# Sample queries: high and low parts side by side in the weight columns, one score pass instead of two

## The chip, the cores and the metric

One core of one Trainium2 chip runs one inference step of a hybrid encoder layer. The metric is the device time of one execution in microseconds (us). Everything is 32-bit; products that need full precision are made of high and low parts in a reduced format (the names ending in hi and lo, or the two halves of a tile called hl).

## The reference, cut to what matters

Two groups of rows go through one layer: 1024 prompt rows and 64 sample rows. The sample rows attend to a cache of 512 past rows and to themselves (8 "fox" heads with a forget bias), and to 256 memory rows (4 memory heads). Only this part is touched by the change:

```
def fox_attend(q, k, v, Fq, Fk, qpos, kpos):
    s = einsum('bqhd,bkhd->bhqk', q, k) * SCALE
    bias = Fq[..., :, None] - Fk[..., None, :]
    s = where(kpos[None, :] <= qpos[:, None], s + bias, NEG)
    p = softmax(s, axis=-1)
    return einsum('bhqk,bkhd->bqhd', p, v)

def mem_attend(qm, mk, mv):
    s = einsum('bqhd,bkhd->bhqk', qm, mk) * SCALE
    p = softmax(s, axis=-1)
    return einsum('bhqk,bkhd->bqhd', p, mv)

# sample rows: fox_attend(q, [ck, k], [cv, v], ...) with 512 + 64 keys, 64 queries
#              mem_attend(qm, cmk, cmv) with 256 keys, 64 queries
```

Around it lie a root-mean-square norm, one input projection, a pooling mixer, SiLU gates, an output projection with residual, and a final norm, for both groups.

## The kernel before, in words

A planner (class Planner, lines 43 to 253) collects all instructions of the kernel in program order, each with a modelled duration, and `flush` puts them into an order: at each step it takes the engine and the instruction that can start first; at equal times TensorE writes into the banks `ps`, `pt` and `po` go ahead of projections. Five engine queues then run in exactly that order. The planner also links the users of a buffer with the users of the next tile that takes the same buffer, and buffers of one tag are handed out in program order. There are two flushes: norms, values, memory keys and the first projections, then all the rest.

Data: `proj` (line 603) makes one 128-column tile of the input projection in three chunks of rows (256, 512 and 320, the last with the 64 sample rows); each chunk is 24 matmuls into a bank of the ring `pp` and an evacuation through a tile of the ring `row`, which has five buffers for the whole kernel (line 292). `q_tile` splits a query tile into high and low halves in a tile `hl` of two halves of 1152 columns, copies the 64 sample columns a second time beside themselves so that they fill 128 weight columns, and stores all four groups of 64 rows to DRAM (`qd`). `load_q` fetches a head's queries into two tiles, `qa` (prompt rows 0 to 511 and the doubled sample rows) and `qb`.

Attention: a head's keys (`ks`, or `km` for a memory head) lie as high part over low part on the 128 partitions, and the queries twice, so one matmul gives a product with both parts of the keys. `score` (line 834) runs two such passes into one bank, with the high and with the low half of the queries as weights. The scores go through the ring `s`, two banks, handed out in program order. `fox_sample` makes scores in two pieces of 288 keys, adds the bias and takes a running minimum on VectorE, takes the exponential on ScalarE, and `sample_pv` transposes 128 rows and multiplies with the values. Rows 64 to 127 repeat rows 0 to 63. `mem_sample` does the same with one piece of 256 keys and no bias. `fox_unit` and `mem_unit` treat four blocks of 256 prompt rows.

Order in the program: for each head of the list "f0:u0 qm0|f1:qm1|f2:q2 k2|f3:u1|m0:q3|m1:|m2:k3|m3:|f4:gf0 gf1|f5:gf2|f6:gf3 gp0|f7:gp1 gmx0" first the head (its loads, its sample part, its four blocks) and then the projections behind the colon (gates are `gate_tile`, with two `row` tiles per chunk; queries and keys take one). Behind the sample part of f7 and behind each of its blocks, `store_rinv` (line 857) transposes the softmax sums through a bank of the ring `pt` and takes one `row` tile. Then come the output projection's weights (`load_wout`) and nine output tiles (`out_tile`), the sample tile first.

Of the kernel before, what the change touches and what calls it, by code (L numbers as in the profile page):

```python
# [7 lines left out]
F32 = mybir.dt.float32  # L8
F32R = mybir.dt.float32r
BF16 = mybir.dt.bfloat16  # L10
AF = mybir.ActivationFunctionType
ALU = mybir.AluOpType
AX = mybir.AxisListType
# [16 lines left out]
CH = [(0, 256), (256, 512), (768, 320)]  # L30
LAST = (2, 1, 0)
NQ = NT + NSA
TQ, TK, TGF, TU, TGP, TQM, TGM = 0, 4, 8, 12, 14, 16, 18


# [237 lines left out]
def tile_hymba_step(  # L273
# [23 lines left out]
    def nm(s):  # L297
        uid[0] += 1
        return f"{s}_{uid[0]}"
# [10 lines left out]
    def row(name):  # L310
        return rp.tile([P, 512], F32, tag="row", name=nm(name))
# [4 lines left out]
    def mm(out, lhsT, rhs, start, stop):  # L316
        nc.tensor.matmul(out, lhsT=lhsT, rhs=rhs, start=start, stop=stop)
# [1 line left out]
    def half(par):  # L319
        return slice(64 * par, 64 * par + 64), slice(64 - 64 * par, 128 - 64 * par)  # L320

    qd = [dram.tile([4 * HD, 2, NQ], F32, name=f"qd{j}") for j in range(6)]
    kd = [dram.tile([4 * HD, NT + PAST], F32, name=f"kd{j}") for j in range(4)]
    md = [dram.tile([4 * HD, 2 * MEM], F32, name=f"md{j}") for j in range(2)]
    gated = [dram.tile([768, n], F32, name=f"gated_{t0}") for t0, n in CH]
# [291 lines left out]
    def halves():  # L617
        return rp.tile([P, 2, NQ], F32R, tag="hl", name=nm("hl"), bufs=HB)

    def split(hl, src, c0, n):  # L620
        hi, lo = hl[:, 0, c0 : c0 + n], hl[:, 1, c0 : c0 + n]
        nc.scalar.copy(hi, src)
        nc.gpsimd.tensor_tensor(lo, src, hi, op=ALU.subtract)

    def q_tile(j):
        hl = halves()

        def f(acc, ci, t0, n):
            t = row("qr")
            nc.vector.scalar_tensor_tensor(  # L630
                t[:, :n], acc[:, :n], SCALE, rb[:, t0 : t0 + n], op0=ALU.mult, op1=ALU.mult
            )
            if ci == 2:
                nc.vector.tensor_copy(t[:, n : n + NSA], t[:, n - NSA : n])
            for a, b, c in ((0, 512, 0), (512, NPR, P), (NPR, NQ, -512)):
                a, b = max(a, t0), min(b, t0 + n + (NSA if ci == 2 else 0))
                if a < b:
                    split(hl, t[:, a - t0 : b - t0], a + c, b - a)
            if ci == 2:
                for r in range(4):  # L640
                    nc.sync.dma_start(qd[j][r * HD : r * HD + HD], hl[r // 2 :: 2].bitcast(F32))

        return f

# [168 lines left out]
    def small(shape, tag):  # L813
        return ap_.tile(shape, F32, tag=tag, name=nm(tag), bufs=6)
# [5 lines left out]

    def load_q(j, par):
        out = []
        for tag, c0, n in (("qa", 0, 512 + P), ("qb", 512 + P, 512)):
            q = ap_.tile([P, 2, n], F32R, tag=tag, name=nm(tag), bufs=1)
            nc.sync.dma_start(q.bitcast(F32), qd[j][par * P : par * P + P, :, c0 : c0 + n])
            out.append(q)
        return out

    def q_part(q, c):
        t = q[c in (2, 3)]  # L830
        c0, n = ((0, 256), (256, 256), (0, 256), (256, 256), (512, P))[c]
        return t[:, 0, c0 : c0 + n], t[:, 1, c0 : c0 + n]

    def score(out, q, qs, kst, ks0, n):
        mm(out, q[0][:, qs], kst[:, ks0 : ks0 + n], True, False)
        mm(out, q[1][:, qs], kst[:, ks0 : ks0 + n], False, True)
# [9 lines left out]
    def softmax_tail(Pt, m, rows, n, rs, src=None):  # L846
        nc.scalar.activation(
            Pt[:rows, :n], Pt[:rows, :n] if src is None else src, AF.Exp, bias=m,
            scale=-1.0 if src is None else 1.0, accum_out=rs[:rows],
        )  # L850
# [3 lines left out]
    def rs_col(c, head, i=0):  # L854
        return rsum[:, c, 12 * i + head : 12 * i + head + 1]
# [104 lines left out]
    def fox_sample(h, ks, raw, q):  # L960
        par = h % 2
        j = h // 2
        n = PAST + NSA
        nb = nbt(5 * P)
        nc.sync.dma_start(
            nb[:, : 5 * P],
            gsd[5 * h : 5 * h + 5, :].rearrange("t p -> (t p)").unsqueeze(0).to_broadcast([P, 5 * P]),
        )
        nc.gpsimd.tensor_tensor(nb[:, PAST:n], nb[:, PAST:n], mask[:, :NSA], op=ALU.add)
        q = q_part(q, 4)  # L970
        Pt = ptile()
        nc.gpsimd.memset(Pt[:, n : n + NSA], 0.0)
        prev = BIG
        for a in (0, 288):
            s = pst()
            score(s[:, :288], q, slice(0, P), ks, NPR + a, 288)
            m = small([P, 1], "m")
            nc.vector.tensor_tensor_reduce(
                out=Pt[:, a : a + 288], in0=s[:, :288], in1=nb[:, a : a + 288],
                scale=-1.0, scalar=prev, op0=ALU.add, op1=ALU.min, accum_out=m,  # L980
            )
            prev = m
        softmax_tail(Pt, prev, P, n, rs_col(4, h))
        sample_pv(Pt, 5, raw, 7, par, j * P)

    def sample_pv(Pt, nt, raw, v0, par, row0):
# [68 lines left out]
    def mem_sample(h, km, raw, q):  # L1055
        par = h % 2
        j = h // 2
        q = q_part(q, 4)
        s = pst()
        score(s[:, :256], q, slice(0, P), km, MEM, 256)  # L1060
        m = small([P, 2], "m2")
        nc.vector.tensor_reduce(
            out=m[:, 0:1], in_=s[:, :256], axis=AX.X, op=ALU.max, negate=True
        )
        Pt = ptile(256)
        softmax_tail(Pt, m[:, 0:1], P, 256, rs_col(4, 8 + h), src=s[:, :256])
        sample_pv(Pt, 2, raw, 1, par, 768 + j * P)

    UW = 15 + NPR + 15 + NSA
# [81 lines left out]
    def out_prep(t):  # L1151
        m = P if t < 8 else NSA
        ci = 0 if t < 2 else 1 if t < 6 else 2
        o, oc = t * P - CH[ci][0], t % 2 * P
        kv = lambda x: x[:, :D].rearrange("p (k t) -> p k t", k=KT)
        hk = lambda x, w: x[:, : w * m].rearrange("p (k t) -> p k t", k=w)
        spare = order.index(t) % 3 == 2
        if spare:
            ch = ap_.tile([P, KT, P], F32R, tag="vs", name=nm("chi"))
        else:  # L1160
            ch = kv(wp.tile([P, WC], F32R, tag="whi", name=nm("chi")))
        if t < 8:
            if spare:
                cl = ap_.tile([P, KT, P], F32R, tag="vs", name=nm("clo"))
            else:
                cl = kv(wp.tile([P, WC], F32R, tag="wlo", name=nm("clo")))
        else:
            cl = ch[:, :, m:]
        w = 512 // m
        if order.index(t) % 2:  # L1170
            rt = ap_.tile([P, 2, 512 + P], F32, tag="qa", name=nm("rt"), bufs=1)
            rt = rt.rearrange("p a b -> p (a b)")
        else:
            rt = ap_.tile([P, 13, HD], F32, tag="vraw", name=nm("rt"), bufs=1)
            rt = rt.rearrange("p a b -> p (a b)")
        rt = rt[:, : 6 * m].rearrange("p (k t) -> p k t", k=6)
        for par in (0, 1):
            nc.sync.dma_start(
                rt[64 * par : 64 * par + 64],
                rsd[min(t // 2, 4)].rearrange("(i k a) t -> i a k t", i=2, a=2)[  # L1180
                    t % 2, par, :, :m
                ].unsqueeze(0).to_broadcast([64, 6, m]),
            )
        for a in range(0, KT, w):
            ct, gt = hk(ptile(512), w), hk(ptile(512), w)
            nc.sync.dma_start(
                ct, catd[t // 2][a * P : (a + w) * P, oc : oc + m].rearrange("(k p) t -> p k t", p=P)
            )
            e1 = min(a + w, 6)
            nc.sync.dma_start(  # L1190
                gt[:, : e1 - a, :],
                gated[ci][a * P : e1 * P, o : o + m].rearrange("(k p) t -> p k t", p=P),
            )
            ks = slice(a, a + w)
            for b0, b1, o0 in ((0, 4, 0), (6, 8, 2)):
                b0, b1 = max(a, b0), min(a + w, b1)
                if b0 < b1:
                    c_ = ct[:, b0 - a : b1 - a, :]
                    nc.vector.tensor_tensor(c_, c_, rt[:, b0 - o0 : b1 - o0, :], op=ALU.mult)
            c_ = ct[:, : e1 - a, :]  # L1200
            nc.gpsimd.tensor_tensor(c_, c_, gt[:, : e1 - a, :], op=ALU.mult)
            if a + w > 6:
                for i in (0, 1):
                    c_ = ct[:, 6 - a + i, :]
                    nc.gpsimd.tensor_tensor(
                        c_, c_, kept[0][:, i, t * P : t * P + m], op=ALU.mult
                    )
            nc.scalar.activation(ch[:, ks, :m], ct, AF.Copy, scale=0.5)
            nc.vector.scalar_tensor_tensor(
                cl[:, ks, :m], ct, 0.5, ch[:, ks, :m], op0=ALU.mult, op1=ALU.subtract  # L1210
            )
        return ch, cl
# [277 lines left out]
```

## Time and profile before

| | |
|---|---|
| median of 3 runs | 597.59 us (596.21 to 597.65) |
| profiled execution, device time | 598.18 us |
| its span from the first to the last instruction | 596.4 us |
| TensorE matmul busy | 567.7 us (95% of the span) |
| TensorE weight loads busy | 519.5 us (87%) |
| VectorE / ScalarE / GpSimd busy | 334.9 / 291.5 / 225.8 us (56 / 49 / 38%) |
| DMA queue of SyncE | 65.4% of the 16 DMA engines' span |

PE is TensorE's matmul, PEld its weight load, DVE VectorE, ACT ScalarE, POOL GpSimd, SP the engine that issues nearly all DMAs. Matmuls are pipelined, so the length of one is not what it costs: that is the distance from one start to the next. A group of n matmuls whose bar is b long, each m long by itself, has starts (b - m) / (n - 1) apart. Nearly all instructions carry the planner's line 252; groups are told apart by tile names and shapes.

### The profile page before, as it was taken

The numbers are of one execution on the slowest core, as the hardware profiler recorded it, in microseconds if no ns is written. First come the engines' busy times: TensorE is split into PE (matmuls) and PEld (weight loads), VectorE is DVE, ScalarE is ACT, GpSimd is POOL, SyncE is SP. The second block draws the span as 40 slices with busy tenths as digits, with TensorE's granted clock in tenths as the row PEclk, the third lists the DMA queues.
The fourth block names the chain that finished last, engine by engine and source line by source line (L and its number), as shares of the span: only waits on it lengthen the run. The fifth ranks groups of instructions, "written<-read, shape, count | busy, mean of one in ns | idle before, by whom it ended". The sixth has DMA issues, their size and how long they took to land.

```text
span 596.4 us, 11206 instructions
## 1 busy us (share of the span) xinstructions
PE 567.7 (95%) x3815; PEld 519.5 (87%) x3815; DVE 334.9 (56%) x822; ACT 291.5 (49%) x675; POOL 225.8 (38%) x374
## 2 busy tenths in 40 slices
PE   7789999999999999999999998999999988999993
PEld 5789999889999999989999988989898767989983
DVE  5774431113677877666498753863356284656334
ACT  5564631122686877787468633862233242323212
POOL 2302374354755542024276560412312294242200
PEclk9999999999999999999999999999999998999998
DMA  8998754568997985586858757824265436585541
GB/s 302 325 312 304 233 162 155 195 233 276 306 341 246 332 263 165 145 320 205 281 162 301 259 160 251 247 88 140 78 169 135 139 106 172 152 259 177 170 142 71
DMA packets 96450, 126.36 MB, mean 212 GB/s; under 512 B 30434, under 2 KB 68618, under 8 KB 94858
## 3 DMA queue, kind: packets, MB, share of 16 engines
q1 hardware_dynamic: 96106, 125.39, 65.4%
q8 instruction: 30, 0.49, 0.3%
q10 hardware_dynamic: 288, 0.27, 0.1%
q14 instruction: 26, 0.21, 0.1%
HBM read 86.41 MB, written 39.21 MB: 211 GB/s over the span
## 4 chain that ended last, share of the span: by engine, by line
PE 77%; DMA 8%; POOL 4%; DVE 4%; issue 3%; ACT 2%; SPq 1%; DVEq 0%; ACTq 0%; POOLq 0%
PE pp L252 38%; PE s L252 15%; PE o L252 13%; PE pt L252 12%; DMA nat<-in_xn_dram 4%; POOL wl L252 2%; DMA rt<-rsd 1%; POOL wlo L252 1%; DMA kd<-hl 1%; DMA xr<-in_xT_dram 1%; DMA ks<-kd 1%; SPq L252 1%; DVE s L252 1%; POOL s L252 1%; DVE xt L252 0%
## 5 line engine op out<-in xcount | busy, mean ns | idle before, releaser
L252 PE MATMUL pp<-xh,whi 128*128 128x320 f32 (+2 forms) x480 | 149.4, 334 | 3.3 <-DVE kr L252 1.6
L252 PE MATMUL pp<-xh,wlo 128*128 128x512 f32 (+2 forms) x480 | 148.1, 332 | 0.0
L252 PE MATMUL pp<-xl,whi 128*128 128x320 f32 (+2 forms) x480 | 147.8, 329 | 0.0
L252 POOL TENSOR_TENSOR wlo<-wr,whi 128x512 fp32r<-128x512 f32 (+2 forms) x44 | 60.3, 1390 | 104.3 <-ACT whi L252 87.8
L252 PEld LDWEIGHTS pp<-xh,whi 128*128 128x128 f32 x480 | 88.3, 188 | 11.2 <-DVE gr L252 2.2
L252 PEld LDWEIGHTS pp<-xh,wlo 128*128 128x128 f32 x480 | 88.2, 188 | 6.0
L252 PEld LDWEIGHTS pp<-xl,whi 128*128 128x128 f32 x480 | 88.5, 189 | 5.0
L252 DVE TENSOR_TENSOR plo<-pt,phi 128x512 fp32r<-128x512 f32 (+1 forms) x96 | 60.6, 642 | 19.6 <-ACT phi L252 15.2
L252 ACT CAST phi<-pt 128x512 fp32r<-128x512 f32 (+1 forms) x96 | 51.8, 550 | 31.7 <-PE pt L252 18.9
L252 PE MATMUL o<-plo,vs 128*128 128x256 f32 x160 | 50.1, 325 | 0.9 <-DVE plo L252 0.9
L252 ACT CAST whi<-wr 128x1024 fp32r<-128x1024 f32 (+1 forms) x25 | 24.6, 983 | 51.7 <-PE pp L252 49.4
L252 PE MATMUL o<-phi,vs 128*128 128x256 f32 x160 | 47.6, 305 | 0.0
L252 PE MATMUL pt<-ident,Q 128*128 128x128 f32 x248 | 47.4, 272 | 0.0
L252 ACT ACTIVATE Q<-Q,m 128x576 f32<-128x576 f32 (+4 forms) x40 | 38.0, 950 | 13.4 <-DVE m L252 13.3
L252 PE MATMUL s<-ks,qb 128*128 128x512 f32 (+3 forms) x128 | 37.9, 374 | 0.5 <-DVE m L252 0.4
L252 POOL TENSOR_TENSOR P<-P,P 128x512 f32<-128x512 f32 (+2 forms) x17 | 18.9, 1114 | 49.0 <-DMA P<-catd 27.8
L252 PEld LDWEIGHTS pt<-ident,Q 128*128 128x128 f32 x248 | 32.2, 140 | 3.1
L252 PEld LDWEIGHTS o<-plo,vs 128*128 128x128 f32 x160 | 30.3, 189 | 2.2 <-DVE plo L252 1.3
L252 PEld LDWEIGHTS o<-phi,vs 128*128 128x128 f32 x160 | 30.3, 189 | 1.4
L252 DVE CUSTOM_DVE_ANT_0 Q<-s,nc 128x512 f32<-128x512 f32 (+2 forms) x40 | 24.0, 601 | 11.4 <-PE s L252 8.1
L252 DVE TENSOR_TENSOR gr<-pp,rb 128x512 f32<-128x512 f32 (+2 forms) x24 | 12.6, 533 | 31.4 <-PE pp L252 31.3
L252 PE MATMUL pt<-ident,P 128*128 128x128 f32 x152 | 28.9, 272 | 0.0
(255 smaller groups left out, 1368.1 us busy)
## 6 DMA issues: line engine op xcount, KB each, us to landing
qd<-hl SPq DMA_DIRECT2D x24, 576.0 KB, 5.2
wr<-in_wt_dram SPq DMA_DIRECT2D x20, 512.0 KB, 3.8
qa<-qd SPq DMA_DIRECT2D x12, 640.0 KB, 5.3
ks<-kd SPq DMA_DIRECT2D x8, 800.0 KB, 5.7
qb<-qd SPq DMA_DIRECT2D x12, 512.0 KB, 4.2
P<-catd SPq DMA_DIRECT2D x17, 256.0 KB, 3.9
nat<-in_xn_dram SPq DMA_DIRECT2D x8, 512.0 KB, 7.6
kd<-hl SPq DMA_DIRECT2D x16, 256.0 KB, 5.1
```

The costliest lines, as they stand in the source:

```text
L252: getattr(getattr(self.nc, op.eng), op.fn)(*op.args, **op.kw)
```

## The change

The sample queries are no longer doubled. Their high and low parts lie side by side in the 128 weight columns, so one pass gives 64 rows of scores with the high parts and 64 rows with the low parts, which are then added. For a fox head ScalarE copies the lower 64 rows to a `row` tile, GpSimd adds the bias to it, and VectorE's reduction takes the upper rows from the bank and the tile as its second input. For a memory head ScalarE copies into the probability tile, VectorE adds, and the maximum is read from there. The unused rows of the probability tiles are set to zero by GpSimd. The stored queries are narrower (2176 columns instead of 2304) and in an order in which each of the two loads is one contiguous run per row.

```
--- before.py
+++ after.py
@@ -30,6 +30,7 @@
 CH = [(0, 256), (256, 512), (768, 320)]
 LAST = (2, 1, 0)
 NQ = NT + NSA
+QW = 2 * NT
 TQ, TK, TGF, TU, TGP, TQM, TGM = 0, 4, 8, 12, 14, 16, 18
 
 
@@ -319,7 +320,7 @@
     def half(par):
         return slice(64 * par, 64 * par + 64), slice(64 - 64 * par, 128 - 64 * par)
 
-    qd = [dram.tile([4 * HD, 2, NQ], F32, name=f"qd{j}") for j in range(6)]
+    qd = [dram.tile([4 * HD, QW], F32, name=f"qd{j}") for j in range(6)]
     kd = [dram.tile([4 * HD, NT + PAST], F32, name=f"kd{j}") for j in range(4)]
     md = [dram.tile([4 * HD, 2 * MEM], F32, name=f"md{j}") for j in range(2)]
     gated = [dram.tile([768, n], F32, name=f"gated_{t0}") for t0, n in CH]
@@ -624,21 +625,25 @@
 
     def q_tile(j):
         hl = halves()
+        fl = hl.rearrange("p a b -> p (a b)")
 
         def f(acc, ci, t0, n):
             t = row("qr")
             nc.vector.scalar_tensor_tensor(
                 t[:, :n], acc[:, :n], SCALE, rb[:, t0 : t0 + n], op0=ALU.mult, op1=ALU.mult
             )
-            if ci == 2:
-                nc.vector.tensor_copy(t[:, n : n + NSA], t[:, n - NSA : n])
-            for a, b, c in ((0, 512, 0), (512, NPR, P), (NPR, NQ, -512)):
-                a, b = max(a, t0), min(b, t0 + n + (NSA if ci == 2 else 0))
+            for a0, b0, h0, l0 in ((0, 512, 0, 640), (512, NPR, 1152, 1664), (NPR, NT, 512, 576)):
+                a, b = max(a0, t0), min(b0, t0 + n)
                 if a < b:
-                    split(hl, t[:, a - t0 : b - t0], a + c, b - a)
+                    hi = fl[:, h0 + a - a0 : h0 + b - a0]
+                    lo = fl[:, l0 + a - a0 : l0 + b - a0]
+                    nc.scalar.copy(hi, t[:, a - t0 : b - t0])
+                    nc.gpsimd.tensor_tensor(lo, t[:, a - t0 : b - t0], hi, op=ALU.subtract)
             if ci == 2:
                 for r in range(4):
-                    nc.sync.dma_start(qd[j][r * HD : r * HD + HD], hl[r // 2 :: 2].bitcast(F32))
+                    nc.sync.dma_start(
+                        qd[j][r * HD : r * HD + HD], fl[r // 2 :: 2, :QW].bitcast(F32)
+                    )
 
         return f
 
@@ -820,16 +825,18 @@
 
     def load_q(j, par):
         out = []
-        for tag, c0, n in (("qa", 0, 512 + P), ("qb", 512 + P, 512)):
-            q = ap_.tile([P, 2, n], F32R, tag=tag, name=nm(tag), bufs=1)
-            nc.sync.dma_start(q.bitcast(F32), qd[j][par * P : par * P + P, :, c0 : c0 + n])
+        for tag, c0, n in (("qa", 0, 1024 + P), ("qb", 1024 + P, 1024)):
+            q = ap_.tile([P, n], F32R, tag=tag, name=nm(tag), bufs=1)
+            nc.sync.dma_start(q.bitcast(F32), qd[j][par * P : par * P + P, c0 : c0 + n])
             out.append(q)
         return out
 
     def q_part(q, c):
-        t = q[c in (2, 3)]
-        c0, n = ((0, 256), (256, 256), (0, 256), (256, 256), (512, P))[c]
-        return t[:, 0, c0 : c0 + n], t[:, 1, c0 : c0 + n]
+        t, a, b = q[c // 2], c % 2 * 256, (640, 512)[c // 2] + c % 2 * 256
+        return t[:, a : a + 256], t[:, b : b + 256]
+
+    def q_pair(q):
+        return q[0][:, 512:640]
 
     def score(out, q, qs, kst, ks0, n):
         mm(out, q[0][:, qs], kst[:, ks0 : ks0 + n], True, False)
@@ -967,20 +974,25 @@
             gsd[5 * h : 5 * h + 5, :].rearrange("t p -> (t p)").unsqueeze(0).to_broadcast([P, 5 * P]),
         )
         nc.gpsimd.tensor_tensor(nb[:, PAST:n], nb[:, PAST:n], mask[:, :NSA], op=ALU.add)
-        q = q_part(q, 4)
+        q = q_pair(q)
         Pt = ptile()
-        nc.gpsimd.memset(Pt[:, n : n + NSA], 0.0)
+        nc.gpsimd.memset(Pt[:NSA, n : n + NSA], 0.0)
+        nc.gpsimd.memset(Pt[NSA:, : 5 * P], 0.0)
         prev = BIG
         for a in (0, 288):
             s = pst()
-            score(s[:, :288], q, slice(0, P), ks, NPR + a, 288)
-            m = small([P, 1], "m")
+            mm(s[:, :288], q, ks[:, NPR + a : NPR + a + 288], True, True)
+            b = nb[:NSA, a : a + 288]
+            t = row("sl")[:NSA, :288]
+            nc.scalar.copy(t, s[NSA:, :288])
+            nc.gpsimd.tensor_tensor(t, t, b, op=ALU.add)
+            m = small([P, 1], "m")[:NSA]
             nc.vector.tensor_tensor_reduce(
-                out=Pt[:, a : a + 288], in0=s[:, :288], in1=nb[:, a : a + 288],
+                out=Pt[:NSA, a : a + 288], in0=s[:NSA, :288], in1=t,
                 scale=-1.0, scalar=prev, op0=ALU.add, op1=ALU.min, accum_out=m,
             )
             prev = m
-        softmax_tail(Pt, prev, P, n, rs_col(4, h))
+        softmax_tail(Pt, prev, NSA, n, rs_col(4, h))
         sample_pv(Pt, 5, raw, 7, par, j * P)
 
     def sample_pv(Pt, nt, raw, v0, par, row0):
@@ -1055,15 +1067,16 @@
     def mem_sample(h, km, raw, q):
         par = h % 2
         j = h // 2
-        q = q_part(q, 4)
         s = pst()
-        score(s[:, :256], q, slice(0, P), km, MEM, 256)
-        m = small([P, 2], "m2")
-        nc.vector.tensor_reduce(
-            out=m[:, 0:1], in_=s[:, :256], axis=AX.X, op=ALU.max, negate=True
-        )
+        mm(s[:, :256], q_pair(q), km[:, MEM : 2 * MEM], True, True)
         Pt = ptile(256)
-        softmax_tail(Pt, m[:, 0:1], P, 256, rs_col(4, 8 + h), src=s[:, :256])
+        nc.gpsimd.memset(Pt[NSA:, :256], 0.0)
+        t = Pt[:NSA, :256]
+        nc.scalar.copy(t, s[NSA:, :256])
+        nc.vector.tensor_tensor(t, s[:NSA, :256], t, op=ALU.add)
+        m = small([P, 2], "m2")[:NSA, 0:1]
+        nc.vector.tensor_reduce(out=m, in_=t, axis=AX.X, op=ALU.max, negate=True)
+        softmax_tail(Pt, m, NSA, 256, rs_col(4, 8 + h), src=t)
         sample_pv(Pt, 2, raw, 1, par, 768 + j * P)
 
     UW = 15 + NPR + 15 + NSA
@@ -1168,8 +1181,7 @@
             cl = ch[:, :, m:]
         w = 512 // m
         if order.index(t) % 2:
-            rt = ap_.tile([P, 2, 512 + P], F32, tag="qa", name=nm("rt"), bufs=1)
-            rt = rt.rearrange("p a b -> p (a b)")
+            rt = ap_.tile([P, 1024 + P], F32, tag="qa", name=nm("rt"), bufs=1)
         else:
             rt = ap_.tile([P, 13, HD], F32, tag="vraw", name=nm("rt"), bufs=1)
             rt = rt.rearrange("p a b -> p (a b)")
```

## Rows read from the trace of the kernel before

**Rows 1.** The page: busy time of the engines, and PE in 40 slices.
```profile
PE 567.7 (95%) x3815; PEld 519.5 (87%) x3815; DVE 334.9 (56%) x822; ACT 291.5 (49%) x675; POOL 225.8 (38%) x374
...
PE   7789999999999999999999998999999988999993
```

**Rows 2.** Busy time by stretch: each engine's us and instructions, granted clock, DMA.
```profile
0.00:50.00 50.00, 41.51 (x284) 37.02 (x285) 33.79 (x77) 29.87 (x59) 11.46 (x12) 1.00 0.94 318
...
150.00:200.00 50.00, 49.85 (x351) 46.13 (x349) 37.83 (x120) 37.71 (x91) 31.64 (x63) 1.00 0.92 293
200.00:236.00 36.00, 36.00 (x277) 34.27 (x276) 27.60 (x84) 27.47 (x68) 13.66 (x40) 1.00 0.76 250
236.00:280.00 44.00, 43.85 (x315) 40.94 (x314) 28.84 (x55) 34.43 (x107) 8.65 (x13) 1.00 0.68 218
...
400.00:430.00 30.00, 30.00 (x178) 26.95 (x177) 9.90 (x16) 7.63 (x12) 7.49 (x6) 1.00 0.31 102
430.00:460.00 30.00, 28.79 (x201) 26.71 (x201) 16.64 (x35) 11.21 (x20) 8.01 (x8) 1.00 0.54 152
460.00:500.00 40.00, 35.35 (x174) 28.41 (x174) 23.30 (x27) 14.37 (x22) 21.06 (x17) 0.96 0.50 145
...
550.00:597.00 47.00, 36.79 (x235) 33.05 (x233) 17.99 (x48) 9.24 (x27) 6.53 (x8) 0.93 0.40 133
```

**Rows 3.** Groups by shape, matmuls: names, shape, count | busy us, mean ns | idle before.
```profile
L252 PE MATMUL s<-ks,qa 128*128 128x288 f32 x32 | 6.7, 301 | 1.5 <-DMA ks<-kd 1.5
L252 PE MATMUL s<-km,qa 128*128 128x256 f32 x40 | 6.6, 282 | 0.0
```

**Rows 4.** Timeline around the first sample part: start, length, engine, instruction, count.
```profile
151.58 0.70 PE L252 MATMUL s<-ks,qa 128*128 128x288 f32 x4
...
152.05 0.46 DVE L252 CUSTOM_DVE_ANT_0 Q<-s,nc 128x288 f32<-128x288 f32 x1 [2.85 <-PE s L252]
...
152.69 0.52 DVE L252 CUSTOM_DVE_ANT_0 Q<-s,nc,m 128x288 f32<-128x288 f32 x1 [0.17 <-DVE m L252]
...
153.14 0.40 PE L252 MATMUL s<-ks,qa 128*128 128x256 f32 x2
```

**Rows 5.** Groups by shape on ACT, POOL and DVE that stand nearest to the edits.
```profile
L252 ACT COPY ot<-o 64x256 f32<-64x256 f32 x48 | 17.7, 368 | 7.1 <-PE o L252 6.0
...
L252 POOL TENSOR_TENSOR s<-s 64x256 f32<-64x256 f32 x4 | 3.0, 741 | 0.3
...
L252 POOL MEMSET Q<- 128x64 f32 x8 | 1.2, 153 | 3.7 <-PE pt L252 2.5 <-PE o L252 1.2
...
L252 POOL MEMSET tall<- 128x200 f32 x1 | 0.3, 266 | 0.0
...
L252 DVE TENSOR_TENSOR cat<-o,ot 64x256 f32<-64x256 f32 x48 | 20.0, 419 | 10.5 <-ACT ot L252 7.7 <-DMA catd<-cat 2.3
...
L252 DVE COPY qr<-qr 128x64 f32<-128x64 f32 x6 | 2.4, 398 | 0.1
...
L252 DVE TENSOR_REDUCE m<-s 128x1 f32<-128x256 f32 x4 | 1.7, 420 | 2.1 <-PE s L252 2.1
```

**Rows 6.** DMA issues: transfer, count, KB each, median us to landing.
```profile
qa<-qd SPq DMA_DIRECT2D x12, 640.0 KB, 5.3
...
qb<-qd SPq DMA_DIRECT2D x12, 512.0 KB, 4.2
```

**Rows 7.** Timelines of PE and DVE, 401 to 435: f7's sums and the gates.
```profile
401.76 0.27 PE L252 MATMUL pt<-ident,rinv 128*24 128x128 f32 x1
...
402.33 0.63 PE L252 MATMUL pp<-xh,whi 128*128 128x512 f32 x2
...
430.96 0.69 DVE L252 TENSOR_TENSOR gr<-pp,rb 128x512 f32<-128x512 f32 x1 [0.82 <-PE pp L252]
...
433.35 0.27 DVE L252 COPY rt<-pt 24x128 f32<-24x128 f32 x1
...
434.27 0.20 DVE L252 COPY rt<-pt 12x64 f32<-12x64 f32 x1
```

## The prediction

> **What bounds the kernel now.** I read the page's busy times first, then the stretches, then the groups by shape, and last two timelines. TensorE's matmuls cover 567.7 of 596.4 us, and in the page's 40 slices PE stands at 9 nearly throughout, with two dips at the ends and one near slice 32 [rows 1]. The stretches say it more sharply: from 200 to 236 us PE is busy 36.00 of 36.00 us, from 236 to 280 us 43.85 of 44, and this is where heads run [rows 2]. The largest idle shares are at the start (8.5 us of the first 50), between 430 and 500 us (1.2 + 4.65 us) and at the end (10.2 us) [rows 2]. All other engines have room in the attention stages: between 150 and 200 us DVE is busy 37.83, ACT 37.71 and POOL 31.64 of 50 us [rows 2]. So in the stages that the change touches, the wait that ends last is TensorE's own queue: whatever is taken from PE there is worth its price, as long as PE has something else to run while a head waits. That something is the projections. From 400 to 430 us the engine runs hardly anything else, 178 matmuls in 30.00 busy us [rows 2], 0.169 us each, so a projection tile of 72 matmuls is worth about 12 us of cover.
>
> **The change, part by part.** *Score matmuls.* A fox head's sample part has four matmuls of 288 columns, a memory head's two of 256. The count of the first is 32 [rows 3], and half goes: 16. Four go from the memory heads (4 of the 40 of that group, which also holds blocks of prompt rows [rows 3]). Four of 288 take a bar of 0.70 us where one takes 0.301 [rows 3, 4], so starts are (0.70 - 0.30) / 3 = 0.133 us apart; two of 256 take 0.40 us where one takes 0.28 [rows 3, 4], 0.12 us apart. Removed from PE: 16 x 0.133 + 4 x 0.12 = 2.6 us. Nothing is added on PE: transposes and value products stay as they were, on 128 rows.
>
> *The sum of halves.* Per fox head two copies of 64 x 288 on ACT, two adds of 64 x 288 on POOL; the reduction on DVE keeps its length, since it has as many columns as before. By columns from the nearest rows, a copy is 0.368 x 288 / 256 = 0.41 us and an add 0.741 x 288 / 256 = 0.83 us (both estimates from [rows 5]). ACT gains 16 x 0.41 + 4 x 0.37 (memory heads) = 8.0 us, POOL 16 x 0.83 = 13.3 us, DVE 4 x 0.42 = 1.7 us. The zeros: 64 columns take 153 ns and 200 take 266 [rows 5], so 0.83 ns a column; 640 columns are 0.52 us, 256 columns 0.20 us, with the fixed 0.1 us each 8 x 0.62 + 4 x 0.31 = 6.2 us of POOL. On engines busy 49 and 38% [rows 1] I cost these at nothing. What hides them is TensorE's queue of projections. Without that cover it is latency that counts, and that is the term to be bounded. Before, the first piece's reduction begins 0.47 us after its first matmul, and 1.56 us after it the next block's first score runs in the same bank [rows 4]. After, a copy and an add lie between (0.41 + 0.83 = 1.24 us, with two handovers of some 0.15 us 1.5 us). The second piece's add queues behind the first's and ends with it within a similar delay. So each fox head's scores are put off by about 1.5 us, and since the ring `s` has two banks handed out in order, all scores behind them. A memory head's copy and add replace nothing: 0.37 + 0.42 = 0.8 us. Ends: 0 us (all covered) and 8 x 1.5 + 4 x 0.8 = 15.2 us (none covered). Below zero it can't be by itself, as it only adds work. I take 0: in the stretches with heads, PE is idle for 0.15 us in 50, 0 in 36 and 0.15 in 44 [rows 2], although DVE has waits of its own in the same place (2.85 us before the first reduction [rows 4]), so the cover there is demonstrated.
>
> By the Trainium skill ("Perfetto Trace Analysis", section on matmuls), independent groups should rotate through different PSUM banks so that the evacuation of one lies beside the matmuls of the next. That speaks against this part, as two banks are now held longer; by it alone the sum would go towards the upper end.
>
> *Queries.* Six copies on DVE of 64 columns go (6 x 0.40 = 2.4 us [rows 5]), beside an engine at 56% [rows 1]: nothing. Each of the 12 loads of `qa` shrinks from 640 KB (landing after 5.3 us [rows 6]) to 576, those of `qb` stay at 512 KB (4.2 us [rows 6]); runs of 2560 and 2048 bytes become runs of 4608 and 4096. They're issued while the head before is running. Bounds: 0, and at most a quicker landing by half for the 12 loads of `qa`, 2.6 us each, but only where a head's first score waits for it; matmuls of `qa` show a wait for keys alone, 1.5 us [rows 3]. I take 0.
>
> *The row ring.* The new `row` tiles join a ring of five in program order, and so tie heads to projections. It can be seen in the trace what that ring does: the sums of f7's first block are transposed at 401.76, but are copied out at 433.35 and 434.27 only when gp0's gates leave their buffers (its evacuations at 430.96 and after) [rows 7]. For 31.6 us both banks of `pt` stood, f7's later blocks waited, and PE ran projections. After, f3's sample scores need q2's last chunks, f4's q3's, f5's gf1's first, f6's gf2's and f7's gp0's second chunk. That moves heads behind projections that before ran later than the heads did. PE's work stays the same; its order doesn't. Bounds: nothing where projections remain to run beside the head, which holds for f3 to f6 (at least one tile, 12 us, each). For f7 there remain gp0's last chunk, two chunks of gp1 and one of the gates behind, some 17 us of projection beside some 14 us of its own matmuls. I take 0 with both signs open: up to -5.9 us, if the idle time from 430 to 500 us closes, and up to the term above.
>
> **Sum.** The profiled execution took 598.18 us, span 596.4 and 1.8 around it. 598.18 - 2.6 = 595.6 us. It lies 0.6 us above the median of the runs shown (597.59), so against that I forecast 597.59 - 2.6 = 595.0 us.
>
> **Rivals.** *A, not PE.* If TensorE's busy time isn't what sets the end, 20 matmuls less change nothing: 597.6 us. For it: weight loads are busy 87% [rows 1], which leaves 13% that matmuls don't use. Against it: in the timeline, starts follow each other at 0.133 us for 288 columns [rows 4], with no gap beside the columns' own time at the granted clock of 1.00 (its upper level, 2.4 GHz) [rows 2], and the weight loads run under them. The gain can also be lost where the order is made anew, by some tenths of a per cent either way. By the Trainium skill ("Trainium Kernel Development and Optimization", performance expectations), matmul busy time is a bad measure of the distance from the roofline and weight-load busy time a good one; by that, 13% would be slack and this rival's 597.6 us the answer.
>
> *B, the uncovered chain (slower).* The place is the last fox heads, above all f7, whose scores now start only behind gp0's second chunk. If PE has used up its projections by then, the longer hold of the two `s` banks shows. Price: half of the 15.2 us uncovered is 7.6 - 2.6 = +5.0, 602.6 us; the point from which it decides is 2.6 of the 15.2 us uncovered, a sixth. For it: two banks of `pt` already stood for 31.6 us by the same ring [rows 7], and between 430 and 460 us PE is at 28.79 of 30 and then at 35.35 of 40 [rows 2]. Against: in every stretch with heads the cover holds [rows 2].
>
> *C, the ring helps (faster by more).* Heads and projections in step leave fewer projections for a late block of their own (400 to 430 us [rows 2]) and more of f7 to run between the last gates, where PE is idle 5.9 us and its clock falls to 0.96 of full [rows 2]. Half of that, 3 us, gives 592.0 us.
>
> **How the numbers follow.** Forecast (593.2 to 596.8 us) 0.4, A 0.2, B 0.2, C 0.2. Under 0.3% (1.8 us) a measurement of this kernel can't tell from no change. Faster by more than that (below 595.8) are C and most of the forecast's own range: 0.52. Within 0.3%: A and the forecast's upper part, 0.27. Slower: B and a little of A, 0.21. The range reaches into C and B until a fifth is left out: 589.0 to 602.0 us.
>
> **What would show it.** The 288-column group of `s` should count 16 instead of 32, and PE's busy time be 2.6 us less. A gap of PE just ahead of `s` matmuls, waiting for DVE's reduction, ACT's copy or POOL's add, would show B; the first scores of f7 should stand behind gp0's second gate evacuation in any case, and if they don't, I've misread the ring. If PE's idle time between 430 and 500 us shrinks by 2 us or more, C is at work. The prediction is wrong if PE's busy time falls as said and the end doesn't follow; then PE wasn't the bound.

## The result, and the profile after

The changed kernel takes 598.8 us (median of 20 runs, 594.99 to 601.56), the kernel before 596.8 us in the same session (20 runs, 595.18 to 598.12). The ratio is 1.0035, 95% interval 1.002 to 1.0049: slower by 2.1 us, where 2.6 us less were forecast. The profiled execution of after took 598.84 us.

The page after: its span, PE's busy time, PE and the granted clock in 40 slices.

```profile
span 597.0 us, 11202 instructions
...
PE 568.6 (95%) x3795; PEld 519.0 (87%) x3795; DVE 339.2 (57%) x820; ACT 298.1 (50%) x695; POOL 240.4 (40%) x402
...
PE   7899999999999999999998999999999978999993
...
PEclk9899999999999999999999999999999989999998
```

PE runs 20 matmuls fewer than in [rows 1] and yet is busy 0.9 us longer. The groups of after (name, shape, count | busy us, mean ns of one | idle before) show that the edits did what they say and at what price:

```profile
L253 PE MATMUL s<-km,qa 128*128 128x256 f32 x36 | 6.5, 289 | 0.0
...
L253 PE MATMUL s<-ks,qa 128*128 128x288 f32 x16 | 4.5, 294 | 0.0
...
L253 ACT COPY sl<-s 64x288 f32<-64x288 f32 x16 | 6.1, 391 | 3.1 <-PE s L253 1.9 <-DVE gr L253 1.1
...
L253 POOL TENSOR_TENSOR sl<-sl,nc 64x288 f32<-64x288 f32 x16 | 13.1, 825 | 4.9 <-ACT sl L253 3.0 <-DVE pl L253 1.8
...
L253 POOL MEMSET Q<- 64x640 f32 x8 | 5.0, 630 | 4.3 <-PE o L253 2.5 <-PE pt L253 1.4
```

The counts 16 and 36 stand for 32 and 40 in [rows 3]. A copy takes 0.391 us (0.41 estimated), an add 0.825 (0.83), a memset of 640 columns 0.630 (0.62). The stretches (busy us of each engine, granted clock, DMA share and GB/s) answer to [rows 2]:

```profile
200.00:236.00 36.00, 35.71 (x264) 33.91 (x263) 21.04 (x64) 21.66 (x53) 15.47 (x35) 1.00 0.57 182
236.00:280.00 44.00, 43.35 (x300) 39.30 (x300) 27.36 (x64) 31.10 (x88) 14.07 (x28) 1.00 0.76 253
280.00:320.00 40.00, 38.89 (x279) 36.30 (x278) 31.01 (x72) 30.96 (x92) 25.15 (x38) 1.00 0.72 238
320.00:360.00 40.00, 38.12 (x258) 35.08 (x257) 21.75 (x53) 19.89 (x44) 16.38 (x33) 1.00 0.68 205
...
430.00:460.00 30.00, 29.49 (x201) 26.74 (x200) 19.99 (x59) 16.51 (x37) 8.17 (x12) 1.00 0.62 176
460.00:500.00 40.00, 35.89 (x172) 29.26 (x172) 22.06 (x27) 13.93 (x23) 19.74 (x18) 0.91 0.48 145
500.00:550.00 50.00, 48.39 (x340) 44.96 (x340) 29.71 (x59) 15.77 (x35) 15.78 (x20) 1.00 0.67 190
```

From 430 to 500 us the idle time fell from 5.9 us [rows 2] to 4.6. New gaps stand elsewhere: 0.3 us in 200 to 236 and 1.6 us in 500 to 550, where there were none, and 3.6 us in 236 to 360, where there were 1.6. The kernel before, in the stretches that [rows 2] leaves out:

```profile
280.00:320.00 40.00, 39.62 (x289) 37.58 (x288) 29.25 (x84) 27.02 (x70) 22.52 (x41) 1.00 0.76 231
320.00:360.00 40.00, 38.98 (x267) 35.54 (x267) 25.19 (x60) 22.51 (x51) 22.54 (x44) 1.00 0.73 249
...
500.00:550.00 50.00, 50.00 (x345) 46.35 (x345) 28.54 (x63) 14.20 (x34) 15.13 (x20) 1.00 0.63 178
```

The timeline shows what holds the heads (start, length, engine, instruction; idle time before it in brackets). This is f5:

```profile
335.71 0.29 PE L253 MATMUL s<-ks,qa 128*128 128x288 f32 x1
...
336.54 0.29 PE L253 MATMUL s<-ks,qa 128*128 128x288 f32 x1
...
352.20 0.42 DVE L253 TENSOR_TENSOR gr<-pp,rb 128x256 f32<-128x256 f32 x1 [0.46 <-PE pp L253]
...
353.04 0.38 ACT L253 COPY sl<-s 64x288 f32<-64x288 f32 x1
...
354.86 0.99 POOL L253 TENSOR_TENSOR sl<-sl,nc 64x288 f32<-64x288 f32 x1
...
355.88 0.45 DVE L253 CUSTOM_DVE_ANT_0 Q<-s,sl 64x288 f32<-64x288 f32 x1 [0.70 <-POOL sl L253]
...
363.61 2.86 DVE L253 SCALAR_TENSOR_TENSOR gr<-gt,gr 128x512 f32<-128x512 f32 x2 [0.96 <-ACT gt L253]
...
365.00 0.40 ACT L253 COPY sl<-s 64x288 f32<-64x288 f32 x1 [1.06 <-DVE gr L253]
...
370.74 0.50 DVE L253 CUSTOM_DVE_ANT_0 Q<-s,sl,m 64x288 f32<-64x288 f32 x1
```

Both score matmuls are done by 337 us, but their copies start at 353.04 and 365.00, among the gate tiles (`gr`, `gt`) behind which the ring puts them, and the second reduction ends at 371.2. For 35.5 us f5 has at least one bank of `s`, and both of them for 19.8 us, until its first reduction ends at 356.3. f3 holds a bank 22.2 us (216.28 to 238.5, both for 2.7) and f7 24.0 us (409.26 to 433.3, both for 16.4; copies at 423.64 and 430.65); the other heads 3.9 to 9.8 us. Before, no head held one longer than 3.9 us; f5 then:

```profile
314.58 0.43 PE L252 MATMUL s<-ks,qa 128*128 128x288 f32 x2
...
315.15 0.45 DVE L252 CUSTOM_DVE_ANT_0 Q<-s,nc 128x288 f32<-128x288 f32 x1
...
315.25 0.42 PE L252 MATMUL s<-ks,qa 128*128 128x288 f32 x2
...
315.81 0.52 DVE L252 CUSTOM_DVE_ANT_0 Q<-s,nc,m 128x288 f32<-128x288 f32 x1 [0.20 <-PE s L252]
```

"Hold" below is this time, from a head's first sample matmul to the end of its second reduction.

### The profile page after: what moved, and what is told of

Same layout as the page of the kernel before. It is cut to its first block, busy times and chain, and to the rows that moved or that the text cites. A ratio compares the mean times of both kernels' runs of the same rounds, so it can differ in the third digit from the quotient of the medians.

```text
span 597.0 us, 11202 instructions
## 1 busy us (share of the span) xinstructions
PE 568.6 (95%) x3795; PEld 519.0 (87%) x3795; DVE 339.2 (57%) x820; ACT 298.1 (50%) x695; POOL 240.4 (40%) x402
## 4 chain that ended last, share of the span: by engine, by line
PE 77%; DMA 9%; DVE 5%; issue 3%; ACT 3%; POOL 2%; SPq 0%; DVEq 0%; ACTq 0%; POOLq 0%
PE pp L253 42%; PE s L253 13%; PE o L253 12%; PE pt L253 11%; DMA nat<-in_xn_dram 2%; DMA catd<-cat 2%; DMA xr<-in_xT_dram 1%; DMA vraw<-out_dram 1%; POOL wl L253 1%; DMA wr<-in_wv_dram 1%; DVE plo L253 1%; DMA out_dram<-u 1%; DVE s L253 1%; ACT phi L253 1%; DVE gr L253 1%
## 5 line engine op out<-in xcount | busy, mean ns | idle before, releaser
L253 PE MATMUL pp<-xh,whi 128*128 128x256 f32 (+2 forms) x480 | 150.0, 332 | 1.6 <-DVE kr L253 0.9
L253 PE MATMUL pp<-xl,whi 128*128 128x320 f32 (+2 forms) x480 | 150.3, 330 | 0.0
L253 PE MATMUL pp<-xh,wlo 128*128 128x320 f32 (+2 forms) x480 | 149.0, 331 | 0.5 <-POOL wlo L253 0.5
L253 POOL TENSOR_TENSOR wlo<-wr,whi 128x512 fp32r<-128x512 f32 (+2 forms) x44 | 60.1, 1385 | 62.3 <-ACT whi L253 55.4
L253 ACT ACTIVATE Q<-Q,m 64x576 f32<-64x576 f32 (+4 forms) x40 | 37.9, 948 | 17.6 <-DVE m L253 17.3
L253 ACT CAST whi<-wr 128x1024 fp32r<-128x1024 f32 (+1 forms) x25 | 24.5, 980 | 34.1 <-PE pp L253 32.0
L253 ACT ACTIVATE chi<-P 128x512 fp32r<-128x512 f32 x17 | 10.6, 631 | 39.6 <-POOL P L253 23.2
L253 ACT ACTIVATE P<-P,m 128x128 f32<-128x128 f32 (+4 forms) x36 | 20.0, 556 | 15.4 <-DVE m L253 15.2
```

What stands on the lines that cost most here:

```text
L253: getattr(getattr(self.nc, op.eng), op.fn)(*op.args, **op.kw)
```

## The experiments

Three readings were open. First, the ring of five `row` buffers ties heads to projections and costs the time. Second, the longer chain (copy, add, reduction) costs it, ring or not. Third, nothing of the change costs it: any edit makes the planner write another order, some orders are slow, and the output phase with its lower clock decides. Each expectation was written before its run. "Margin" is the constant of 0.4 that both flushes hand to the planner; another value gives another order of the same instructions.

**The kernel before again**, unchanged, for its times and clocks.

> The kernel before, unchanged, so that each of its runs comes with its granted clock. Theory T1 (the 2.6 us of score matmuls were gained before the output phase and given back in it, by idle time of PE and by TensorE's clock falling to its lower level after that): the clock of these runs is 0.990 to 0.994 in most, clearly above that of the changed kernel's runs (0.977 to 0.991), and ratio 1.000. Rival T2 (the longer chain of the sample scores, with two banks held, costs the time in the attention stages): the clocks of the two kernels don't differ enough to matter; the same ratio 1.000.

596.55 us in 12 runs, ratio 1.001 (0.9994 to 1.0026). Its granted clocks are 0.983 to 0.995 but for one run, its times 593.72 to 597.87 without a relation to them (593.72, 597.04 and 597.87 all at 0.989). One run at 0.944 took 596.43. So in the kernel before the clock, expected to tell the kernels apart, shows no relation to the time. In after it does: of the 20 runs the three at 0.989 to 0.991 took 594.99 to 596.38 us, no more than the kernel before, and the 17 at 0.977 to 0.986 took 597.60 to 601.56. So a part of after's time may be the clock's, as the third reading has it; the runs below bound that part.

**Narrow layout, two passes of 64 columns**: the new queries and loads without copy, add and `row` tile, and without the saving on PE.

```
-    return q[0][:, 512:640]
+    return q[0][:, 512:576], q[0][:, 576:640]
...
-    mm(s[:, :288], q, ks[:, NPR + a : NPR + a + 288], True, True)
...
+    score(s[:NSA, :288], q, slice(0, NSA), ks, NPR + a, 288)
```

> The changed kernel with its narrow query layout, but with two score passes of 64 weight columns that accumulate in the bank: no copy, no add, no row tile for the sample scores. PE gets the 2.6 us of matmuls back. T2 says this is as fast as before or faster (596 to 597), since the chain is gone, and clearly faster than the changed kernel. T1 says the time hangs on how the output phase falls out, not on the chain: anywhere from 595 to 600 us, and in its trace the last projection matmul ends about where it did before (482.5 us) and not at 480.4.

595.71 us, 1.0001 (0.9987 to 1.0015); PE busy 567.5 us. In this order, storing, loading and zeroing in the new way costs nothing, as forecast; one order can't show it closer than the orders below scatter.

**The sum in place**: copy and add as in after, but in the probability tile itself.

```
-            t = row("sl")[:NSA, :288]
+            t = Pt[:NSA, a : a + 288]
```

> The changed kernel, but the low halves are copied straight into the probability tile and the bias is added there, so that no tile of the row ring is used: heads are not tied to projections. T2, in the form that the row ring does the harm: 594 to 595 us (the forecast's 2.6 us come through), banks of s held no longer than 3 us. T1: the banks are free as well, but the time again hangs on the output phase: 595 to 600 us, with the last projection at 480 to 481 us.

590.04 us, 0.9904 (0.9882 to 0.9927). No hold is above 9.8 us, PE is busy 562.6 us, and the last projection matmul ends at 473.7 us instead of 480.4. That is 4 us below the 594 to 595 expected, with holds longer than the 3 us expected. The chain of copy, add and reduction is all there, and no kernel of the case was faster, which speaks against the second reading.

**Sixteen matmuls of 512 columns more**, ahead of the third output tile, to fill the gap in which after loses its clock.

```
+            if t == order[2] and o == 0 and w == 512:
+                for _ in range(16):
+                    mm(acc[:, :512], whi[0][:, 0, :P], whi[0][:, 0, :512], True, True)
```

> The changed kernel with 16 extra matmuls of 128x512 (3.7 us of PE) on the output weights, put into the bank of the third output tile ahead of its real matmuls, which overwrite it; they stand in PE's queue in the stretch where PE was idle (486 to 490 us). T1 with the clock as the second half of the loss: PE isn't idle there, the clock stays at its upper level behind it, mean clock 0.988 to 0.992 and 594 to 597 us although there is more work. T2 or a pure change of order: 3.7 us more work of which some falls into idle time, so the same to 2 us slower than the changed kernel's 598.8 us.

597.19 us, 1.0029 (1.0002 to 1.0055), not to be told from after's 1.0035. The run is inconclusive: the granted clock stays at 1.00 until 500 us, but falls to 0.97 from 500 to 550 us, so the stretch at the lower level moved rather than went, and the added matmuls have a price of their own. What the clock was worth in the profiled executions stands in the last section.

**The ring without the change**: the kernel before, its bias copied into a `row` tile for each 288 keys.

```
+            t = row("sl")[:, :288]
+            nc.gpsimd.tensor_copy(t, nb[:, a : a + 288])
...
-                out=Pt[:, a : a + 288], in0=s[:, :288], in1=nb[:, a : a + 288],
+                out=Pt[:, a : a + 288], in0=s[:, :288], in1=t,
```

> The kernel before, with both score passes, but the bias of each 288 keys is first copied by GpSimd into a tile of the row ring, and the reduction reads that. No matmul goes and no copy stands between the score and the reduction; only the tie of the ring is added (and 16 copies of some 0.6 us on GpSimd). T2 (the row ring does the harm; in the run without it the change was 5.7 us faster than before): the harm comes alone, 3 to 9 us slower than before, 599 to 605 us, and banks of s are held for tens of us by the heads f3, f5 and f7. T1 (the order of the whole falls out by luck): no reason for slower, 594 to 598 us.

598.62 us, 1.0045 (1.0014 to 1.0076), just under the 599 to 605 expected; holds of 22.2 (f3), 40.2 (f5) and 25.1 us (f7). Its timeline at f5:

```profile
330.24 0.42 PE L252 MATMUL s<-ks,qa 128*128 128x288 f32 x2
...
354.86 0.62 POOL L252 COPY sl<-nc 128x288 f32<-128x288 f32 x1
...
366.25 0.69 POOL L252 COPY sl<-nc 128x288 f32<-128x288 f32 x1
...
369.89 0.51 DVE L252 CUSTOM_DVE_ANT_0 Q<-s,sl,m 128x288 f32<-128x288 f32 x1
```

The same pattern as in after, from the tile alone: the matmuls at 330, the copies at 354.86 and 366.25, though these copies need no score. The 16 copies are work of their own, and no run has them in a buffer outside the ring.

**Other orders.** Before, after and in place at margins of 0.35 and 0.45 (`MARGIN = 0.4` replaced).

> The kernel before with the planner's margin 0.35 instead of 0.4: the same work in another order on all engines, as a measure of what order alone does. T1: 2 us or more away from before, either way (594 or 598). T2: within 1.5 us of before (594.2 to 597.2), since nothing that ties heads to projections changes.

> The changed kernel with the margin 0.35. T2: still slower than the in-place form by 5 us or more, so 595 to 600 us. T1: anything from 590 to 600 us.

> The in-place form (no row tile for the sample scores) with the margin 0.35. T2: the gain stays, 588.5 to 592.5 us. T1: the 590.0 us at 0.4 was one lucky order; back at 594 to 598 us.

> The kernel before with the planner's margin 0.45. T2 (the row ring does the harm): within 1.5 us of before. T1 (order by luck): 2 us or more away, either way.

> The changed kernel with the margin 0.45. T2: 4 us or more above the in-place form at the same margin. T1: anything from 590 to 600 us.

> The in-place form with the margin 0.45. T2: the gain stays, 588.5 to 592.5 us. T1: 594 to 598 us.

Ratios to the kernel before at margin 0.4, on each run's own chip:

| margin | before | after | in place |
|---|---|---|---|
| 0.35 | 0.9945 (0.9928 to 0.9963) | 1.0034 (1.0007 to 1.0061) | 0.9953 (0.9922 to 0.9984) |
| 0.40 | 1 | 1.0035 (1.002 to 1.0049) | 0.9904 (0.9882 to 0.9927) |
| 0.45 | 1.0052 (1.0029 to 1.0074) | 1.0035 (1.0006 to 1.0064) | 0.9909 (0.9873 to 0.9946) |

The third reading has a part in it: order alone moves the kernel before from 592.99 to 600.25 us, where the first reading expected it to stay within 1.5 us. In place at 0.35 took 593.13 us instead of at most 592.5, no less than the kernel before in that order. But after is above in place in every row, by 0.008, 0.013 and 0.013, that is 4.8 to 7.8 us (5 or more were expected at 0.35, the 4.8); and its holds recur (21.7, 34.1 and 25.3 us at 0.35; 20.2, 35.8 and 20.3 at 0.45), while in place has none above 9.8.

**A buffer of its own.** In place removes the extra tile too. So after once more, with the tile kept and only taken out of the ring (one buffer, so that the second copy waits for the first reduction), at two margins; and the ring without the change at the other margins.

```
-            t = row("sl")[:NSA, :288]
+            t = rp.tile([P, 288], F32, tag="sl", name=nm("sl"), bufs=1)[:NSA]
```

> The kernel after, with the copied half rows in one buffer of their own (tag sl, one buffer for the whole kernel) instead of a tile of the ring row; copy, add and reduction as after, and the second piece's copy now waits until the first piece's reduction has read the buffer. Theory (the ring's tie costs the time): no head holds its two s banks for more than 10 us, last projection matmul by 477 us, time 589 to 594 us. Rival (the tile and its longer chain cost it, the ring does not): 597 to 601 us, holds as in the kernel after or shorter, time not below the kernel before.

> The same with the planner's margin at 0.35 instead of 0.4, that is another order. Theory: 590 to 595 us, below the kernel after at this margin (597.9 us). Rival: 597 to 601 us.

> The kernel before with its bias copied into a row tile for each 288 keys, margin 0.35. Theory (the tie costs some 3 to 6 us in any order): above the kernel before at this margin (593.0 us) by 2 us or more, 595 to 600 us, holds over 20 us in at least one head. Rival (order alone): 593 us within 1.5 us.

> The same at margin 0.45. Theory: not below the kernel before at this margin (600.3 us), 600 to 605 us. Rival (order alone): anywhere between 593 and 601 us, with no relation to the holds.

Own buffer: 590.19 us, 0.9918 (0.9891 to 0.9944) and 590.13 us, 0.9914 (0.9891 to 0.9938). The longest holds are 11.4 us, just over the 10 us expected. Against after at the same margins that is 0.0117 and 0.0120 lower, 7 us both times, for one line that changes which buffer the tile gets and, through that, the order, but no work. The ring without the change: 598.99 us, 1.0051 (1.0014 to 1.0088) and 601.55 us, 1.0107 (1.0079 to 1.0135); against before at the same margin it costs 0.0106 and 0.0055, after 0.0045 at 0.40: 2.7 to 6.3 us in all three orders. So in all eight pairs, five with the change and three without, the kernel with the tie is the slower one. That settles that the tie costs time, and the second reading falls. The clock is not all of it: the own buffer's runs at 0.4 (granted clock 0.985 to 0.994) all lie between 589.09 and 592.35 us, below after's three runs at 0.989 to 0.991. f5 with its own buffer, page and timeline:

```profile
PE 562.8 (96%) x3795; PEld 516.2 (88%) x3795; DVE 334.5 (57%) x820; ACT 298.8 (51%) x695; POOL 243.6 (41%) x402
```

```profile
317.28 0.29 PE L253 MATMUL s<-ks,qa 128*128 128x288 f32 x1
...
318.55 0.40 ACT L253 COPY sl<-s 64x288 f32<-64x288 f32 x1
...
322.91 0.98 POOL L253 TENSOR_TENSOR sl<-sl,nc 64x288 f32<-64x288 f32 x1
...
326.09 0.40 ACT L253 COPY sl<-s 64x288 f32<-64x288 f32 x1 [0.60 <-DVE m L253]
...
328.21 0.51 DVE L253 CUSTOM_DVE_ANT_0 Q<-s,sl,m 64x288 f32<-64x288 f32 x1 [0.75 <-POOL sl L253]
```

The first copy starts 1.3 us after the matmul instead of 17.3. The add then starts only 4 us after the copy's end, as GpSimd is busy, and the kernel is fast all the same. Its stretches, where after had its gaps:

```profile
236.00:280.00 44.00, 44.00 (x318) 41.14 (x317) 30.52 (x61) 35.88 (x107) 13.28 (x23) 1.00 0.75 248
280.00:320.00 40.00, 39.89 (x295) 37.96 (x294) 31.19 (x81) 30.55 (x83) 23.68 (x43) 1.00 0.74 239
320.00:360.00 40.00, 39.50 (x278) 36.17 (x277) 27.06 (x69) 24.89 (x58) 23.73 (x47) 1.00 0.83 255
...
460.00:500.00 40.00, 35.39 (x202) 29.34 (x201) 20.69 (x26) 13.29 (x22) 23.11 (x21) 1.00 0.46 133
500.00:550.00 50.00, 50.00 (x330) 45.65 (x329) 28.09 (x62) 13.14 (x33) 14.93 (x19) 1.00 0.72 213
```

**Where the 7 us lie.** A sum over all of PE's starts shows the places. The distance from one matmul's start to the next is split into the earlier one's columns at the upper clock level (2.4 GHz) and the rest. The heads' stage goes from the first score matmul to the last projection matmul.

| us | before | after | own buffer | after, 0.35 | own buffer, 0.35 |
|---|---|---|---|---|---|
| columns, whole kernel | 475.6 | 473.3 | 473.3 | 473.3 | 473.3 |
| rest ahead of the heads' stage | 28.5 | 28.4 | 28.6 | 27.4 | 27.6 |
| rest in the heads' stage | 65.5 | 65.9 | 60.7 | 67.3 | 60.8 |
| rest behind it | 15.5 | 18.3 | 14.7 | 15.3 | 15.9 |
| of the heads' stage: rests over 0.1 us | 14.5 (70) | 15.3 (80) | 9.5 (56) | 15.5 (65) | 9.3 (58) |

The profiled execution of the kernel before lies 1.4 us above its median; profiled again (596.42 us) it has 64.5 us of rest in the heads' stage and 13.3 us (69) in rests over 0.1 us. The columns fall by 2.3 us, near the forecast, and stay gone. In the heads' stage after has 5.2 and 6.5 us more in rests than with a buffer of its own, nearly all in rests over 0.1 us, that is, waits. Most of the difference stands ahead of the heads' own matmuls (banks `s`, `pt` and `o`), with 11.5 us of waits in after and 4.6 with its own buffer, 8.7 and 3.6 at 0.35. Ahead of the bank `pp`, where projections held up by the heads' tiles would show, there are 3.8 and 4.9 us, 6.8 and 5.7 at 0.35. And the waits don't lie in the holds. The three holds of after last 81.8 us together and contain 7 of the 80 waits, 1.9 us; the other 73, 13.4 us, lie in the remaining 248 us. With its own buffer the whole stage of 324 us has 9.5. So while a head is held, PE runs projections with hardly a wait. That these are used up by then, and that the heads which run later have less to run beside their own waits, is a reading of these sums; no run shows it by itself.

The rest behind the stage has a part too. It is 17.7 to 18.6 us in after and in the ring without the change at margins 0.40 and 0.45, and 15.3 us in both at 0.35; in every kernel without the tie it is 14.0 to 15.9 us. So it comes with the tie, but not in every order (the run with 16 more matmuls, which fill a gap there, has 14.5 us). In the ring without the change most of the loss at 0.40 and 0.45 lies there: the rest in its heads' stage is 64.4, 64.9 and 67.3 us at 0.40, 0.35 and 0.45, against 65.5, 62.3 and 67.3 us before, so that the stage itself loses at 0.35 alone. In all six kernels of both forms the last score matmul starts at 444.0 to 445.6 us, in every kernel without the tie at 395.7 to 405.0. How the later heads lengthen what comes after them stays open.

## Why the prediction was wrong, point by point

- *Score matmuls, -2.6 us*: right. Counts 16 and 36, columns 2.3 us less. With the ring out of the way, in place and own buffer lie 4.1 us under the kernel before at the same margin on average over five pairs (-5.7, +0.5, -8.5, -4.9, -1.8 us by the ratios), a scatter that holds 2.6 but can't confirm it to a microsecond.
- *The sum of halves, 0 of 0 to 15.2 us*: right as a term. The three durations were met within 0.02 us. The 1.5 us by which it was to put off a head were too few (with its own buffer a head held the banks 4.0 to 11.4 us, before 1.6 to 3.9), but those kernels are among the fastest.
- *Queries, 0*: right in the one order tried (ratio 1.0001 without the rest). `qa` lands after 3.7 us instead of 5.3 [rows 6], but `qb` after 7.5 instead of 4.2:

```profile
qa<-qd SPq DMA_DIRECT2D x12, 576.0 KB, 3.7
...
qb<-qd SPq DMA_DIRECT2D x12, 512.0 KB, 7.5
```

- *The row ring, 0 "with both signs open"*: this step failed. The tie measured +7 us (7.0 and 7.2 by the own buffer, 4.8 to 7.8 by in place): the change without it lies 4.9 us under the kernel before (own buffer at 0.40), with it 2.1 us above. "That moves heads behind projections" was right: f5's sample matmuls start at 335.71 us instead of 314.58, f7's at 409.26 instead of 383.04. The sign named for it was not met: f7's first scores were to stand behind gp0's second gate evacuation, but the score matmuls ran at 409.26 and 410.02 us and the first copy ahead of that evacuation, only the second behind it:

```profile
423.64 0.38 ACT L253 COPY sl<-s 64x288 f32<-64x288 f32 x1
...
425.35 0.69 DVE L253 TENSOR_TENSOR gr<-pp,rb 128x512 f32<-128x512 f32 x1 [1.16 <-PE pp L253]
...
430.65 0.38 ACT L253 COPY sl<-s 64x288 f32<-64x288 f32 x1
```

So within a head the ring holds up the copies and not the score matmuls, and it is finished scores that stand in the banks of `s`, 20 to 36 us in f3, f5 and f7. The prediction gave this wait no price. "Nothing where projections remain to run beside the head" counted the cover where it was spent (rightly: 1.9 us of waits in 81.8), while the loss stands outside the holds. The 31.6 us in [rows 7] were a sample of such a hold, and three more should have been priced above zero. The range of 589.0 to 602.0 us holds 598.8, but only because it was opened towards rival B.

- *Rival A* (PE isn't the bound) has little for it: in the heads' stage PE waited 9.3 to 15.5 us of some 324 to 331 in the kernels of the table, and the own buffer's gain there is a gain in these waits. PE's busy total doesn't decide it. It fell with the time in the own buffer (562.8 us), but the kernel before at 0.35 took 593.0 us with 568.2 busy and after at 0.45 598.8 us with 565.8. By the Trainium skill ("Trainium Kernel Development and Optimization", performance expectations) matmul busy time is a bad measure of the distance to the roofline and weight-load busy time a good one. The trace agrees on the first, as matmul busy time didn't rank these kernels; weight loads stood at 87 to 88% in all these kernels, slow or fast, and didn't tell them apart either.
- *Rival B* (slower) had the side and, by luck, nearly the size: 602.6 us against 598.8. Its mechanism, the longer chain uncovered in the last heads, isn't the cause; its argument from the two banks of `pt` pointed at it. By the Trainium skill ("Perfetto Trace Analysis", matmuls) independent groups of matmuls should rotate through different PSUM banks, so that the evacuation of one lies beside the next. The trace agrees that a bank was held too long, 35.5 us in f5, but the two copies took 0.38 and 0.40 us of that; most of the rest is their wait for a `row` buffer.
- *Rival C*: the idle time from 430 to 500 us shrank, by 1.3 us, less than the 2 us named as its sign, and was lost again behind 500 us.

## What to carry to other kernels

Before a small scratch tile joins an existing ring, look who has its buffers: in a ring handed out in program order each new tile is tied to whoever took its buffer before, here five tiles ago, and a buffer of its own (1.2 KB a partition here) was worth 7 us. Don't price a hold at nothing because the bound engine has something to run during it: here 81.8 us of holds had 1.9 us of waits in them, and the tie that made them still cost 7 us. Where a planner rewrites the whole order after any edit, run the edit at two or three orders before believing a gain of half a per cent.

## What the runs showed of the hardware that was not expected

In after, the granted clock fell behind idle stretches of PE. It was idle 1.60 us ahead of 487.79 and 1.91 us ahead of 490.20; the next matmuls of 512 columns ran at the lower level (1.2 GHz), 0.63 us long where 0.39 to 0.40 is usual:

```profile
487.79 0.49 PE L253 MATMUL pp<-wh,chi 128*128 128x512 f32 x1 [1.60 <-ACT wh L253]
490.20 0.80 PE L253 MATMUL pt<-wh,chi 128*128 128x512 f32 x1 [1.91 <-ACT chi L253]
490.79 0.63 PE L253 MATMUL pt<-wl,chi 128*128 128x512 f32 x1
...
499.06 0.39 PE L253 MATMUL s<-wh,chi 128*128 128x512 f32 x1
```

Eleven matmuls of 512 columns ran so in after, 8 in before, none with the own buffer at margin 0.40 and 7 at 0.35, whose medians differ by 0.06 us. At some 0.21 us each (an estimate: 512 columns at 1.2 GHz less those at 2.4 GHz) the eleven cost 2.3 us, 0.6 more than the eight of before. These are the profiled executions; after's had a mean granted clock of 0.986, where other runs of it went down to 0.977.
